# The gelu of the expert blocks computed ahead, placed one block later on ScalarE

## The chip, the cores and the metric

The kernel runs on one core of a Trainium2 chip. The metric is device microseconds of one execution, here the median of three runs. The core has five engines that run beside each other, each through its own instructions in order: TensorE (PE in the profile; its weight loads are PEld), VectorE (DVE), ScalarE (ACT), GpSimd (POOL) and SyncE (SP). An engine that waits for a semaphore holds back all that is queued behind it. ScalarE and SP also issue DMAs; those stand in the same queues as their other instructions. TensorE writes its results into PSUM, which ScalarE and VectorE read.

## What is computed

Two trunk layers over 512 latent and 256 context tokens of width 1024: a state-space mixer, then latent attention, each followed by a PEER channel mixer that picks 16 of 16384 experts for each of 8 heads. The change concerns PEER alone:

```
def peer_channel(h, w_q, keys, u_tab, v_tab):
    idx, gate = peer_route(t, w_q, keys)          # 8 heads x 16 experts for each token
    def block(args):
        hb, ib, gb = args
        act = jax.nn.gelu(jnp.einsum('td,tkd->tk', hb, u_tab[ib]), approximate=False) * gb
        return jnp.einsum('tk,tkd->td', act, v_tab[ib])
```

## The kernel before

For four token tiles of 128 tokens in the first layer and three in the second, PEER is computed densely: for each of 128 blocks of 128 experts, s = U h for all these tokens, gelu(s), times a gate matrix that is zero where a token has not picked the expert, times V. The other tiles (two and one) gather their experts' rows by indirect DMA (`gather`, lines 1233 to 1272). U, V and the activations are split into a high and a low fp32r part, so that three products stand for one: `split` (lines 302 to 305) casts the high part on ScalarE (L304) and subtracts on VectorE (L305). Line numbers L304 and L305 in the profile are therefore those of a helper, and the tile's name tells what is cast.

**Blocks ahead.** The products s = U h need neither the routing nor the gates. So 40 blocks of the first layer and 48 of the second (A0, A1) are computed ahead, while the tokens are still being routed and the gate matrices made: `ahead` (L1116 on). For each block it loads U (512 KB, on SP's queue), casts Uh (L304) and makes Ul (L305), runs 24 matmuls into one PSUM tile `s_ps` (L1110), applies the gelu on ScalarE (L1113) and stores the result `ge` to HBM (`ged`, L1123, a DMA issued by ScalarE). `pipeline(steps, LA)` with LA = 2 traces the load and split of block b+2 immediately ahead of the products of block b. In the dense stage `dense` (L1132 on) loads `ged` back (L165) in place of computing the block.

**Beside them.** `route` (L931 on) finds the top 16 on VectorE for each tile, `gate_matrix` (L1031 on) makes one-hots `e` on VectorE (L1053), casts them to `o` on ScalarE (L1058, L1064) and on VectorE (L1061), multiplies them on TensorE into `g_ps` (L1075), copies these out of PSUM on ScalarE (L1077) into `stage` and stores that to `gm` (L1079, a DMA of ScalarE's queue). The dense stage loads `gm` as `Gt`. `merge` interleaves these generators by the costs that they yield. In `peer`, `most` stops the blocks ahead three short of their number (TL = 3); the last three are traced at the beginning of `dense`.

**Order.** A planner turns the traced program into one queue for each engine. It may move an instruction ahead of earlier ones of its engine that its own timing takes to be ready later. `keep_in_program_order(x)` takes that freedom from one instruction: x then comes behind the instruction that was traced just before it on the same engine. All PSUM tiles share one pool of eight buffers (L113); U, Uh, Ul, the one-hots and other 4 KB tiles share a pool of 20.

Of the kernel before, what the change touches and what calls it, by code (L numbers as in the profile page):

```python
# [14 lines left out]
AF = mybir.ActivationFunctionType  # L15
# [70 lines left out]
def pipeline(steps, ahead):  # L86

    got = []
    for n in range(len(steps) + ahead):
        if n < len(steps):  # L90
            got.append(steps[n][0]())
        if n >= ahead:
            yield steps[n - ahead][1](got[n - ahead])
            got[n - ahead] = None
# [12 lines left out]
class Net:  # L107
# [992 lines left out]

    def dense_u(self, Us):

        PE, S = self.nc.tensor, self.nc.scalar
        TD = len(self.tiles) * 128
        Uh, Ul = Us
        sp = self.ps([128, TD], "s_ps")
        n = 0
        for k in range(KD):
            for x, y in ((Uh, 0), (Uh, 1), (Ul, 0)):
                PE.matmul(out=sp, lhsT=x[:, k, :], rhs=self.Hs[:, y, k, :], start=(n == 0), stop=(n == 3 * KD - 1))  # L1110
                n += 1
        ge = self.t2([128, TD], "ge")
        S.activation(out=ge, in_=sp, func=AF.Gelu)  # L1113
        return ge

    def ahead(self, l, n, n_tiles):  # L1116

        NT = len(self.tiles)
        self.n_ahead, self.n_done = n, 0
        self.ged = self.dram.tile([n, 128, NT * 128], F32, name=f"ged{l}")  # L1120

        def work(b, Us):
            self.nc.scalar.dma_start(out=self.ged[b], in_=self.dense_u(Us))  # L1123
            self.n_done = b + 1
            return 5.2 * NT / 4

        while len(self.qT) < n_tiles:
            yield 1.0
        yield from pipeline([(lambda b=b: self.dense_u_prep(l, b, self.nc.vector), lambda Us, b=b: work(b, Us))
                             for b in range(n)], LA)  # L1130

    def dense(self, l):  # L1132

# [453 lines left out]
```

## Time and profile before

| | us |
|---|---|
| median of 3 runs | 4093.73 |
| lowest and highest run | 4090.12, 4096.3 |
| profiled execution | 4102.76 |
| its span, first to last instruction | 4101.0 |

The rows of the profile are those of the one profiled execution. A row of the timeline gives start in us, duration in us, engine, line, operation, output tile and inputs, shapes and number of instructions merged; in brackets stands how long the engine was idle before it and what released it ("<-PE s_ps L1110": the matmul of line 1110 that writes s_ps). A row of the waits list gives the waiting engine, tile and line, whom it waited for, and then microseconds in total, number of times and the longest. A row of the windows gives the stretch and its length in us, the busy us (and instructions) of PE, PEld, DVE, ACT and POOL in this order, the TensorE clock granted as a share of full speed, and the share and GB/s of the DMA engines.

### The profile page before, as it was taken

The numbers are of one execution on the slowest core, as the hardware profiler recorded it, in microseconds if no ns is written. First come the engines' busy times: TensorE is split into PE (matmuls) and PEld (weight loads), VectorE is DVE, ScalarE is ACT, GpSimd is POOL, SyncE is SP. The second block draws the span as 40 slices with busy tenths as digits, with TensorE's granted clock in tenths as the row PEclk, the third lists the DMA queues.
The fourth block names the chain that finished last, engine by engine and source line by source line (L and its number), as shares of the span: only waits on it lengthen the run. The fifth ranks groups of instructions, "written<-read, shape, count | busy, mean of one in ns | idle before, by whom it ended". The sixth has DMA issues, their size and how long they took to land.

```text
span 4101.0 us, 53725 instructions
## 1 busy us (share of the span) xinstructions
PE 3714.2 (91%) x18955; PEld 3028.3 (74%) x18955; DVE 3140.5 (77%) x6364; ACT 1468.5 (36%) x2653; POOL 1205.7 (29%) x940
## 2 busy tenths in 40 slices
PE   6759999888679999999999989998887899999998
PEld 3437768677667878788888855568887778989997
DVE  9784387976867788989898844439977678888888
ACT  1221123366622232233332243323466333333333
POOL 5733000022413455556555300000012113333341
PEclk7879999899989999999999999999999999999999
DMA  5457244377887899999999820144377888887976
GB/s 182 137 172 250 79 132 152 100 238 249 290 311 284 294 336 354 341 358 337 341 335 346 300 98 3 44 157 137 123 239 240 310 274 316 294 339 279 343 288 217
DMA packets 398447, 986.14 MB, mean 240 GB/s; under 512 B 67040, under 2 KB 147424, under 8 KB 393568
## 3 DMA queue, kind: packets, MB, share of 16 engines
q1 hardware_dynamic: 217120, 501.34, 35.3%
q0 software_dynamic: 110592, 402.70, 27.7%
q10 hardware_dynamic: 70464, 78.65, 5.5%
q8 instruction: 149, 2.44, 0.2%
q14 instruction: 122, 1.00, 0.1%
HBM read 892.28 MB, written 90.21 MB: 240 GB/s over the span
## 4 chain that ended last, share of the span: by engine, by line
PE 54%; issue 15%; DVE 14%; POOL 7%; DMA 6%; ACT 2%; SPq 1%; POOLq 0%; ACTq 0%; DVEq 0%
PE s_ps L1110 19%; PE acc L1180 14%; POOL row L1248 6%; PE qp L919 4%; PE op L790 3%; DMA row<-in_peer_v,idx 2%; PE g_ps L1075 2%; PE zp L761 2%; DMA W<-in_peer_v 1%; DVE Ul L305 1%; PE op_mla L1480 1%; DMA ge<-ged 1%; DVE w L644 1%; PE yp L696 1%; DVE Ws L305 1%
## 5 line engine op out<-in xcount | busy, mean ns | idle before, releaser
L1180 PE MATMUL acc<-Ws,A 128*128 128x512 f32 x5208 | 1203.0, 392 | 62.7 <-ACT A L304 39.2
L1110 PE MATMUL s_ps<-Hs,Uh 128*128 128x512 f32 (+1 forms) x4096 | 1186.7, 371 | 9.2 <-ACT Uh L304 9.2
L1180 PEld LDWEIGHTS acc<-Ws,A 128*128 128x128 f32 x5208 | 982.0, 189 | 279.4 <-ACT A L304 40.0
L1248 POOL DMA_INDIRECT row<-in_peer_u,idx x384 | 512.5, 1335 | 2139.8 <-DVE row L1255 1271.8
L1110 PEld LDWEIGHTS s_ps<-Hs,Uh 128*128 128x128 f32 x4096 | 762.6, 190 | 103.8 <-ACT Uh L304 11.1
L1110 PE MATMUL s_ps<-Hs,Ul 128*128 128x512 f32 (+1 forms) x2048 | 758.3, 370 | 20.5 <-DVE Ul L305 20.5
L1248 POOL DMA_INDIRECT row<-in_peer_v,idx x384 | 483.9, 1260 | 548.2 <-DVE f L1260 477.6
L1260 DVE SCALAR_TENSOR_TENSOR f<-row,act,f 128x1024 f32<-128x1024 f32 x381 | 487.2, 1279 | 38.0 <-DMA row<-in_peer_v,idx 36.6
L1255 DVE SCALAR_TENSOR_TENSOR row<-row,m 128x1024 f32<-128x1024 f32 x384 | 461.3, 1218 | 38.8 <-DMA row<-in_peer_u,idx 38.0
L304 ACT CAST Ws<-W 128x512 fp32r<-128x512 f32 x512 | 306.2, 619 | 496.9 <-DMA W<-in_peer_v 443.3
L305 DVE TENSOR_TENSOR Ul<-U,Uh 128x1024 fp32r<-128x1024 f32 x256 | 312.0, 1220 | 175.0 <-ACT Uh L304 172.5
L1110 PEld LDWEIGHTS s_ps<-Hs,Ul 128*128 128x128 f32 x2048 | 389.5, 190 | 71.6 <-DVE Ul L305 24.8
L305 DVE TENSOR_TENSOR Ws<-W,Ws 128x512 fp32r<-128x512 f32 x512 | 345.2, 684 | 109.4 <-ACT Ws L304 108.7
L304 ACT CAST Uh<-U 128x1024 fp32r<-128x1024 f32 x256 | 267.7, 1048 | 299.8 <-DMA U<-in_peer_uT 231.7
L1075 PE MATMUL g_ps<-o,o 128*128 128x128 f32 x1792 | 241.3, 294 | 114.3 <-ACT o L1058 72.0
L1113 ACT ACTIVATE ge<-s_ps 128x512 f32<-128x512 f32 (+1 forms) x256 | 139.1, 544 | 545.8 <-PE s_ps L1110 518.2
L1075 PEld LDWEIGHTS g_ps<-o,o 128*128 128x128 f32 x1792 | 230.7, 207 | 126.1 <-ACT o L1058 124.5
L304 ACT CAST A<-ge 128x512 fp32r<-128x512 f32 (+1 forms) x256 | 144.5, 565 | 262.8 <-DVE ge L1161 257.7
L1161 DVE TENSOR_TENSOR ge<-ge,Gt 128x512 f32<-128x512 f32 (+1 forms) x256 | 155.6, 619 | 74.3 <-ACT ge L1113 48.6
L305 DVE TENSOR_TENSOR A<-ge,A 128x512 fp32r<-128x512 f32 (+1 forms) x256 | 158.3, 619 | 45.2 <-ACT A L304 44.3
L1058 ACT CAST o<-e 128x1024 f32<-128x1024 bf16 x112 | 117.3, 1048 | 88.6 <-DVE e L1053 85.5
L1077 ACT COPY stage<-g_ps 128x512 f32<-128x512 f32 x224 | 125.6, 584 | 62.3 <-PE g_ps L1075 60.8
(332 smaller groups left out, 4034.1 us busy)
## 6 DMA issues: line engine op xcount, KB each, us to landing
U<-in_peer_uT SPq DMA_DIRECT2D x256, 512.0 KB
W<-in_peer_v SPq DMA_DIRECT2D x512, 256.0 KB
gm<-stage ACTq DMA_DIRECT2D x28, 2048.0 KB
ada_wt<-in_ada_w SPq DMA_DIRECT2D x96, 512.0 KB
Gt<-gm SPq DMA_DIRECT2D x16, 2048.0 KB
Gt<-gm SPq DMA_DIRECT2D x16, 1536.0 KB
wq<-in_peer_w_q SPq DMA_DIRECT2D x40, 512.0 KB
wo<-in_s_w_o SPq DMA_DIRECT2D x48, 256.0 KB
```

Of the source, the lines that this page charges most:

```text
L304: self.nc.scalar.copy(out=hi, in_=x)
L305: lo_eng.tensor_tensor(out=lo, in0=x, in1=hi.bitcast(F32), op=ALU.subtract)
L919: PE.matmul(out=st["p"][:, h % 2, i * 128:(i + 1) * 128], lhsT=W[:, k, :], rhs=st[i][:, k, :], start=(k == 0), stop=(k == KD - 1))
L1075: PE.matmul(out=gp[:, t, :], lhsT=o[1][:, t4 * 4 + t, :], rhs=o[0][:, t4 * 4 + t, :], start=True, stop=True)
L1077: S.copy(out=stage[:, :, c:c + 4], in_=gp.rearrange("p t i -> p i t"))
L1110: PE.matmul(out=sp, lhsT=x[:, k, :], rhs=self.Hs[:, y, k, :], start=(n == 0), stop=(n == 3 * KD - 1))
L1113: S.activation(out=ge, in_=sp, func=AF.Gelu)
L1161: V.tensor_tensor(out=gv, in0=gv, in1=Gt[b // SB][:, :, :, b % SB, :], op=ALU.mult)
L1180: PE.matmul(out=acc[hf][d], lhsT=A[b][:, x, c], rhs=Ws[:, y], start=(j == 0 and n == 0), stop=(j == SB - 1 and n == 2))
L1248: GP.indirect_dma_start(out=r, out_offset=None, in_=tab, in_offset=bass.IndirectOffsetOnAxis(ap=ik[:, k:k + 1], axis=0), element_offset=l ...
L1255: x = V.scalar_tensor_tensor(out=r, in0=r, scalar=1.0, in1=m, op0=ALU.mult, op1=ALU.mult, accum_out=act[:, k:k + 1])
L1260: x = V.scalar_tensor_tensor(out=f, in0=r, scalar=act[:, k:k + 1], in1=f, op0=ALU.mult, op1=ALU.add)
```

## The change

The gelu is taken out of `dense_u` into `dense_ge`, the products into `dense_s`. In `ahead`, the gelu of a block and its store are traced behind the products of the next block, and the gelu is kept in program order. The blocks of the dense stage call both in turn as before.

```diff
     def dense_u(self, Us):
 
-        PE, S = self.nc.tensor, self.nc.scalar
+        return self.dense_ge(self.dense_s(Us))[0]
+
+    def dense_ge(self, sp):
+        ge = self.t2(list(sp.shape), "ge")
+        return ge, self.nc.scalar.activation(out=ge, in_=sp, func=AF.Gelu)
+
+    def dense_s(self, Us):
+        PE = self.nc.tensor
         TD = len(self.tiles) * 128
         Uh, Ul = Us
         sp = self.ps([128, TD], "s_ps")
...
-        ge = self.t2([128, TD], "ge")
-        S.activation(out=ge, in_=sp, func=AF.Gelu)
-        return ge
+        return sp
...
+        behind = []
+
+        def gelu(n, sp):
+            ge, x = self.dense_ge(sp)
+            self.tc.keep_in_program_order(x)
+            self.nc.scalar.dma_start(out=self.ged[n], in_=ge)
+
         def work(b, Us):
-            self.nc.scalar.dma_start(out=self.ged[b], in_=self.dense_u(Us))
+            behind.append((b, self.dense_s(Us)))
+            if len(behind) > 1:
+                gelu(*behind.pop(0))
             self.n_done = b + 1
             return 5.2 * NT / 4
...
         yield from pipeline([(lambda b=b: self.dense_u_prep(l, b, self.nc.vector), lambda Us, b=b: work(b, Us))
                              for b in range(n)], LA)
+        gelu(*behind.pop())
```

## Rows read from the trace of the kernel before

**Rows 1.** The page: span, and busy time and share of each engine.

```profile
span 4101.0 us, 53725 instructions
...
PE 3714.2 (91%) x18955; PEld 3028.3 (74%) x18955; DVE 3140.5 (77%) x6364; ACT 1468.5 (36%) x2653; POOL 1205.7 (29%) x940
```

**Rows 2.** Windows: PE, PEld, DVE, ACT and POOL, then clock and DMA.

```profile
660.00:820.00 160.00, 137.34 (x663) 110.59 (x662) 156.53 (x762) 60.10 (x85) 1.88 (x2) 0.93 0.34 104
820.00:1110.00 290.00, 229.03 (x1409) 203.35 (x1408) 215.59 (x258) 191.53 (x349) 84.25 (x56) 0.93 0.77 252
...
1400.00:2300.00 900.00, 896.11 (x3882) 728.98 (x3881) 803.67 (x1021) 273.60 (x417) 493.77 (x378) 1.00 0.94 341
2780.00:2960.00 180.00, 153.06 (x948) 145.64 (x947) 168.20 (x780) 74.46 (x116) 4.70 (x5) 0.92 0.41 133
2960.00:3180.00 220.00, 182.43 (x1215) 179.25 (x1214) 163.30 (x256) 145.25 (x259) 37.71 (x28) 0.95 0.70 231
```

**Rows 3.** Timeline, first layer: last gate store, and the first dense product.

```profile
1108.34 0.37 ACTq L1079 DMA_DIRECT2D gm<-stage  x1
...
1148.76 0.79 PE L1180 MATMUL acc<-Ws,A 128*128 128x512 f32 x1 [24.34 <-ACT A L304]
```

**Rows 4.** Waits of ScalarE, stretches 660:820, 820:1110, 2780:2960 and 2960:3180.

```profile
ACT ge L1113 <- PE s_ps L1110: 64.8, 19, 5.3
...
ACT ge L1113 <- PE s_ps L1110: 35.8, 12, 5.0
...
ACT ge L1113 <- PE s_ps L1110: 42.4, 18, 5.3
...
ACT ge L1113 <- PE s_ps L1110: 24.7, 15, 3.3
```

**Rows 5.** Waits of TensorE, stretches 660:820, 820:1110 and 2780:2960.

```profile
PE s_ps L1110 <- ACT Uh L304: 1.6, 1, 1.6
...
PE g_ps L1075 <- ACT o L1058: 43.8, 31, 6.3
...
PE s_ps L1110 <- ACT Uh L304: 7.6, 4, 2.0
```

**Rows 6.** Timeline, first layer: three pauses of TensorE behind a gelu.

```profile
941.57 0.60 ACT L1113 ACTIVATE ge<-s_ps 128x512 f32<-128x512 f32 x1 [4.99 <-PE s_ps L1110]
...
942.56 1.05 ACT L1058 CAST o<-e 128x1024 f32<-128x1024 bf16 x1 [0.40 <-DVE o L1061]
...
943.66 1.14 PE L1075 MATMUL g_ps<-o,o 128*128 128x128 f32 x5 [2.13 <-ACT o L1058]
...
972.84 2.05 PE L1075 MATMUL g_ps<-o,o 128*128 128x128 f32 x16 [0.83 <-ACT o L1058]
...
1026.50 1.27 PE L1075 MATMUL g_ps<-o,o 128*128 128x128 f32 x9 [0.77 <-ACT o L1058]
```

**Rows 7.** Timeline, second layer: a gelu, the casts behind it, and who waited.

```profile
2845.20 0.49 ACT L1113 ACTIVATE ge<-s_ps 128x384 f32<-128x384 f32 x1 [5.32 <-PE s_ps L1110]
...
2846.09 1.99 ACT L304 CAST Uh<-U 128x1024 fp32r<-128x1024 f32 x2 [0.40 <-ACT ge L1113]
2847.19 0.62 PE L1110 MATMUL s_ps<-Hs,Uh 128*128 128x384 f32 x2 [2.02 <-ACT Uh L304]
...
2858.04 1.22 DVE L305 TENSOR_TENSOR Ul<-U,Uh 128x1024 fp32r<-128x1024 f32 x1 [1.59 <-ACT Uh L304]
```

**Rows 8.** Timeline, first layer: a gelu, and the next Uh cast, which waits for U.

```profile
744.52 0.60 ACT L1113 ACTIVATE ge<-s_ps 128x512 f32<-128x512 f32 x1 [3.53 <-PE s_ps L1110]
...
748.35 1.05 ACT L304 CAST Uh<-U 128x1024 fp32r<-128x1024 f32 x1 [1.66 <-DMA U<-in_peer_uT]
```

**Rows 9.** Timeline: late Uh cast in the gate stretches, first and last pause behind one.

```profile
858.82 1.23 DVE L305 TENSOR_TENSOR Ul<-U,Uh 128x1024 fp32r<-128x1024 f32 x1 [6.89 <-ACT Uh L304]
...
863.53 0.77 PE L1075 MATMUL g_ps<-o,o 128*128 128x128 f32 x2 [5.42 <-ACT o L1058]
...
3170.09 2.28 PE L1075 MATMUL g_ps<-o,o 128*128 128x128 f32 x9 [4.41 <-ACT o L1058]
```

## What I expect, and why

> **What bounds the kernel now.** I read the page first, then the windows of the stages, then the waits of ScalarE and TensorE stretch by stretch, and last the timeline at the places the waits point to. The reader should see in the page that TensorE is busy for 91% of a span of 4101.0 us [rows 1], and in the windows that this average hides two kinds of stage. In the dense product stage (1400 to 2300 us) TensorE works 896 of 900 us at a granted clock of 1.00; nothing that ScalarE does there can shorten it. In the stages where the blocks done ahead lie, it is not full: 137 of 160 us and 229 of 290 us in the first layer, 153 of 180 and 182 of 220 in the second, at granted clocks of 0.92 to 0.95 [rows 2]. Routing and gate matrices run there, with VectorE busy 157 of 160 us while it routes and 216 of 290 us while it makes one-hots. All the work of a stage must be through before the dense products start, and TensorE is full from then on, so what a stage saves arrives at the end of the kernel.
>
> The end of each of these stages is the store of the last gate matrix: the store is issued at 1108.34 us, and the first dense product starts at 1148.76 us after TensorE stood idle for 24.34 us [rows 3]. Three ahead blocks run in between and hide under that wait. So the question is what brings the last gate store forward.
>
> **What the change does, part by part.** Today ScalarE's queue has, per block: cast of U, then the gelu, which sits until the block's 24 products are done, then the store of ged, then the next cast. The waits list puts ScalarE's idle time in front of the gelu at 64.8 us (19 times), 35.8 (12), 42.4 (18) and 24.7 (15) in the four stretches, 167.7 us together [rows 4]. Behind it in the same queue wait the Uh casts, the o casts of the gates, the copies out of PSUM and the stores of gm. The change traces the gelu of block b after the products of b+1 and pins it behind the ScalarE instruction traced just before, which is the Uh cast of b+3 (pipeline with LA = 2 runs prep(b+3) immediately before work(b+1)). It adds no instruction: as many gelus, stores and products as before, 40 blocks and 48. The order of TensorE, VectorE and SP is not named in the change; the loads on SP keep their order, and each ged store on ScalarE's queue moves one block later. The first reader of ged is the dense stage, hundreds of microseconds on for all but the last blocks, so that costs nothing; the last gelu has no later cast to wait for, and the 24.34 us of idle time behind it cover it if it slips by a microsecond [rows 3].
>
> Most of the 167.7 us is free today, because TensorE is working on the very products that ScalarE waits for. Only the part that reaches TensorE counts. I followed each TensorE pause over 0.5 us in the two stages back to what released it, and kept those whose chain goes through a gelu.
>
> First layer. One wait for a Uh cast that stood behind a gelu, 1.62 us [rows 5]. One wait for an o cast: the gelu waits 4.99 us, the o cast follows it at 942.56, and the gate products start at 943.66 after 2.13 us of pause [rows 6]. Two more of that kind, 0.83 and 0.77 us [rows 6]. Sum 1.62 + 2.13 + 0.83 + 0.77 = 5.35 us. The other pauses of the gate stretch, the greater part of 43.8 us [rows 5], have other causes: o casts behind PSUM copies, and one-hots that VectorE made late.
>
> Second layer. Four waits of TensorE for a Uh cast, 7.6 us together [rows 5]. One stands here: gelu at 2845.20 after 5.32 us of waiting, two casts behind it at 2846.09, products at 2847.19 after 2.02 us [rows 7]. With the gelu out of the way both casts could start when their U has landed, well before. Besides, VectorE waits 1.59 us for a Uh cast in front of the last steps of a routing on which the gate transposes wait [rows 7]; I count these 1.6 us once. Sum 7.6 + 1.6 = 9.2 us. These fall while VectorE routes; they count because TensorE takes blocks and gates in one order and has to be through all of them before the last gate product. Were routing alone the pace, the 7.6 would be worth nothing.
>
> Together 5.35 + 9.2 = 14.5 us. Against it stand two costs that the trace does not show, so I bound them. (a) The gelu (0.60 us, and 0.4 us until the next instruction starts behind the store's issue) must still stand somewhere; it may fall in front of an o cast that TensorE wants. At best never, 0; at worst at each of the 27 gelus that wait in the two gate stretches (12 and 15), 27 us. Today, in the first layer, it reached TensorE in 3 places; the value nearest to that is 2 us for both layers, which I take. (b) The gelu now waits behind the landing of U of b+3. ScalarE did once wait 1.66 us for a U to land [rows 8]. While it waits, TensorE has the next block to do; nearest value 0, upper end in the rival on banks below. Net gain 14.5 - 2 = 12.5 us.
>
> The profiled execution took 4102.76 us, 0.22% above the median of 4093.73. I take the 12.5 us from the execution, which gives 4090.3, and the same off the median, which gives **4081 us** (0.3% faster).
>
> **Rivals.**
>
> No change. ScalarE's wait only changes its name. The copies of g_ps out of PSUM stand in the same queue, and TensorE makes g_ps after the products in its own order; so where the gelu waited, the copy waits, and the casts behind it come as late as now. For it: at 941.57 the gelu is released and TensorE goes on at once with work that was queued; most gelu waits cost TensorE nothing. Against it: the four casts in [rows 5, 7] stand behind a gelu directly, with no copy between. The time: 4093.7 less 0 to 6, so 4086 to 4102 with what a new order of the queues may shift.
>
> Faster by more. A Uh cast that comes late makes VectorE wait, then the one-hots, then the o cast, then TensorE: VectorE waits 6.89 us at 858.82 and TensorE 5.42 us at 863.53 [rows 9]. There are eight such pauses over 4 us in the two gate stretches, 45.8 us together; the 5.42 us is the first in time and 4.41 us at 3170.09 the last [rows 9]. If half of that went too, the kernel would gain 23 us more: 4058. Against it: in front of these casts there stands a PSUM copy that waits for TensorE, and the change does not move it.
>
> Slower: PSUM banks. All PSUM tiles share one pool of eight (line 113). Today a block's bank is freed as its products end; afterwards it is held until U of b+3 has landed and been cast. In the stretch at 744.52 the gelu would come behind the cast of 748.35, so at 749.4 instead of 744.5, 4.9 us later [rows 8]: one bank more in use for most of a block's time. From the point at which a ninth bank is asked for, TensorE waits up to 4.9 us, 2.5 on average. This decides from 5 blocks on (5 times 2.5 eats the 12.5 us). If a quarter of the 37 gelus that wait in the two routing stretches (19 and 18) [rows 4] meet it, 9 times 2.5 is 23 us of loss, net 10 slower: 4104; with half of them 4126. For it: routing takes banks in pairs beside the blocks and gates. Against it: the lists of TensorE's waits in the four stretches name the o and Uh casts and VectorE's o and Ul, never a reader of a PSUM tile [rows 5], so banks are not short today. The Trainium skill, page "Perfetto Trace Analysis", section "Optimization Strategy", says that the same gap repeating on the engine that should be saturated can mean that there isn't enough SBUF or PSUM for the next tile; the pauses of this trace differ in length and in releaser, so it does not apply to the kernel before, and by that rule equal pauses in front of the products would be the mark of this rival afterwards.
>
> The change does not do what it says. The pin names one instruction, the one traced before; what is traced later may still go in front, and what stood before may stay. If the casts of b+3 were already in front of the gelus everywhere, nothing would move; the casts that follow a gelu directly [rows 7] speak against it. It would give 4094 and lies within the case of no change.
>
> **How the numbers follow.** Net gain of about 8 to 25 us, the forecast: 0.39. More than that: 0.10. Within 8.2 us of the time before (0.2%, about what a measurement of this kernel can tell from no change): 0.32. Slower by more: 0.19, by banks or by a new order of the queues that is worse by chance. Faster is then 0.39 + 0.10 = 0.49. The range goes from the upper gain, 4058, less 2, to a quarter of the blocks meeting a full pool, 4104, plus 2: 4056 to 4106. Below lie some 0.06 and above some 0.13.
>
> **What would show it.** Right: ScalarE's idle time in front of the gelu in the four stretches falls from 167.7 us to under 40; TensorE's waits for Uh casts of 1.6 and 7.6 us go; the last gate store comes about 4 us earlier in the first layer, and the same store in the second layer about 12 us earlier; the dense stage keeps its length. No change: ScalarE's idle time is found again at the copies of g_ps or at U, and the gate stores come when they did. Banks: TensorE waits for a gelu or a copy that frees a bank. My sum is wrong if the gate store moves by much more or less than the pauses I counted, which would say that a change of order, not the gelu's own wait, decides.

## The result, and the profile after

The changed kernel took 4115.48 us (median of 4 runs, 4114.32 to 4116.36), the kernel before beside it 4095.02 us (4090.12 to 4096.94): a ratio of 1.0052 [1.0034, 1.0069]. It is slower by 20 us, where 4081 us was forecast and 4106 was the upper end of the range. The profiled execution took 4116.36 us.

The page of after shows the same work in a longer span, against [rows 1] (ScalarE has two table loads less):

```profile
span 4114.6 us, 53725 instructions
...
PE 3712.9 (90%) x18955; PEld 3031.1 (74%) x18955; DVE 3136.7 (76%) x6364; ACT 1462.1 (36%) x2651; POOL 1204.2 (29%) x940
```

The waits of ScalarE and TensorE after, in the stretches of [rows 4] and [rows 5] (us in total, times, longest). First ScalarE in 660:820, 820:1110, 2780:2960 and 2960:3180, then TensorE in 820:1110 and 2780:2960:

```profile
ACT ge L1107 <- PE s_ps L1117: 7.0, 3, 3.5
...
ACT stage L1077 <- PE g_ps L1075: 52.1, 66, 4.3
...
ACT ge L1107 <- PE s_ps L1117: 5.1, 5, 2.5
...
ACT stage L1077 <- PE g_ps L1075: 56.2, 48, 5.5
...
PE g_ps L1075 <- ACT o L1058: 43.2, 31, 6.3
...
PE s_ps L1117 <- DVE Ul L305: 17.2, 7, 4.4
...
PE s_ps L1117 <- ACT Uh L304: 0.8, 1, 0.8
```

The change does what it says: ScalarE waits 12.1 us (7.0 + 5.1) for a gelu, where it was 167.7 [rows 4]. But TensorE's wait for the o casts is 43.2 against 43.8 us [rows 5], and the 7.6 us that it waited for Uh casts [rows 5] fell to 0.8 while the wait for VectorE's Ul rose to 17.2 us (11.6 before). In the same four stretches the wait for copies of g_ps rose from 60.7 to 156.3 us. The wait changed its name.

Where the time came in: I followed the starts of the stages in the two profiles. From the first product of the blocks ahead to the last gate store, the first layer took 444.3 us before and 440.9 after. The first dense stage took 1212.9 and 1220.1 us, through longer pauses; a second profile of each (below) has 1212.5 and 1215.9. Of all the profiles taken, the five whose first layer is traced as before have 1210.5 to 1218.2 for this stage, the five with the change's first layer 1212.7 to 1221.0, so whether the change lengthens it can't be told. The second layer took 377.4 and 390.8 us between the same two points, 376.2 and 390.8 in the second profiles: this is the loss, and it repeats. It lies late. Up to the first gate store after is 2 to 5 us ahead; between the fifth and the last gate store it loses 13.5 us:

Windows of TensorE from the fifth to the last gate store of the second layer (columns as in [rows 2]), before and then after:

```profile
3047.35:3177.80 130.45, 106.52 (x734) 104.80 (x733) 93.25 (x105) 89.44 (x163) 26.31 (x19) 0.96 0.77 255
```

```profile
3050.85:3194.80 143.95, 112.83 (x736) 110.49 (x735) 93.26 (x105) 89.98 (x164) 26.42 (x20) 0.92 0.70 228
```

The same 734 products (736 by the records), so 130.45 - 106.52 = 23.9 us idle before and 31.1 after, +7.2; and 6.3 us more busy, as the granted clock, a mean over the stretch, is 0.92 instead of 0.96. Windows cut more finely show where it is low. Before, it stands at the lower of TensorE's two levels (0.50 of full speed, 1.2 instead of 2.4 GHz) in 3104.70:3111.40 and 3169.60:3172.80; after, in 3098.20:3105.00, 3115.30:3122.00, 3166.50:3173.20 and 3187.00:3190.20. TensorE had just stood still each time: its pauses of over 4 us end at 3106.53 and 3170.09 before, and at 3100.87, 3116.32, 3167.31 and 3186.83 after. I call this stretch the last seven gate stores; most of the experiments are read from it.

What the added idle time is can be seen at one block. Timeline of after, from a copy of g_ps on:

```profile
3093.77 0.58 ACT L1077 COPY stage<-g_ps 128x512 f32<-128x512 f32 x1 [3.40 <-PE g_ps L1075]
3094.66 0.58 ACT L1077 COPY stage<-g_ps 128x512 f32<-128x512 f32 x1 [0.31 <-PE g_ps L1075]
3095.14 1.05 ACT L304 CAST Uh<-U 128x1024 fp32r<-128x1024 f32 x1
3096.09 0.49 ACT L1107 ACTIVATE ge<-s_ps 128x384 f32<-128x384 f32 x1
3096.22 1.22 DVE L305 TENSOR_TENSOR Ul<-U,Uh 128x1024 fp32r<-128x1024 f32 x1 [6.98 <-ACT Uh L304]
...
3098.51 1.22 DVE L1053 TENSOR_TENSOR e<-iota,iT 128x2048 bf16<-128x2048 bf16 x1
...
3099.76 1.05 ACT L1058 CAST o<-e 128x1024 f32<-128x1024 bf16 x1 [3.18 <-DVE e L1053]
...
3100.87 1.43 PE L1075 MATMUL g_ps<-o,o 128*128 128x128 f32 x5 [6.24 <-ACT o L1058]
```

The same cast (block 38) in the kernel before:

```profile
3085.61 1.05 ACT L304 CAST Uh<-U 128x1024 fp32r<-128x1024 f32 x1
...
3086.70 1.23 DVE L305 TENSOR_TENSOR Ul<-U,Uh 128x1024 fp32r<-128x1024 f32 x1 [3.25 <-ACT Uh L304]
...
3088.24 0.49 ACT L1113 ACTIVATE ge<-s_ps 128x384 f32<-128x384 f32 x1 [1.58 <-PE s_ps L1110]
...
3089.13 0.59 ACT L1077 COPY stage<-g_ps 128x512 f32<-128x512 f32 x1 [0.40 <-PE g_ps L1075]
3090.03 0.59 ACT L1077 COPY stage<-g_ps 128x512 f32<-128x512 f32 x1 [0.31 <-PE g_ps L1075]
...
3091.61 2.05 PE L1075 MATMUL g_ps<-o,o 128*128 128x128 f32 x16 [1.62 <-ACT o L1058]
```

Before, the cast stands in front of two copies of g_ps and of the gelu. After, it stands behind these two copies, which wait 3.40 us for products that TensorE makes behind a block's 24. VectorE, in order, waits 6.98 us for the cast, the one-hots behind it come late, the cast of o waits 3.18 us for them, and TensorE pauses 6.24 us. Counted through ScalarE's queue, the cast of block 38 stands behind 186 copies before and 188 after, that of block 44 behind 210 and 212; at block 44 the pause is 6.24 us again. In the whole stretch the pauses of 0.5 to 3 us shrink from 13.0 to 8.7 us, as the change meant them to, and those over 3 us grow from 10.95 (6.54 and 4.41) to 22.1 us (6.24, 5.12, 6.24, 4.48). VectorE's and TensorE's queues hold the same operations and tiles in the same order in both kernels from 2962 us on; in this stretch only ScalarE's order differs.

A second thing I had not foreseen stands just ahead of that stretch. Timeline of after:

```profile
3023.17 0.38 ACTq L1079 DMA_DIRECT2D gm<-stage  x1
...
3023.59 1.04 ACT L304 CAST Uh<-U 128x1024 fp32r<-128x1024 f32 x1 [0.45 <-ACT stage L1077]
...
3024.54 0.48 ACT L1107 ACTIVATE ge<-s_ps 128x384 f32<-128x384 f32 x1
...
3025.05 3.79 ACTq L1133 DMA_DIRECT2D ged<-ge  x1
3028.88 0.37 ACT L1043 CAST iT<-tr_ps 128x256 bf16<-128x256 f32 x1 [3.60 <-issue]
...
3029.28 1.23 DVE L1053 TENSOR_TENSOR e<-iota,iT 128x2048 bf16<-128x2048 bf16 x1 [3.40 <-ACT iT L1043]
...
3031.75 1.62 PE L1075 MATMUL g_ps<-o,o 128*128 128x128 f32 x6 [8.90 <-DVE o L1061]
```

The block's store (192 KB) is issued 1.9 us behind that of a gate matrix (2048 KB on the page) and takes ScalarE 3.79 us instead of the usual 0.33. The transposed indices wait, and TensorE pauses 8.90 us where it was 5.42 before:

```profile
3028.01 1.83 PE L1075 MATMUL g_ps<-o,o 128*128 128x128 f32 x7 [5.42 <-DVE o L1061]
```

### The profile page after: what moved, and what is told of

Its sections match the earlier page's. It is cut to its first block, busy times and chain, and to the rows that moved or that the text cites. A ratio compares the mean times of both kernels' runs of the same rounds, so it can differ in the third digit from the quotient of the medians.

```text
span 4114.6 us, 53725 instructions
## 1 busy us (share of the span) xinstructions
PE 3712.9 (90%) x18955; PEld 3031.1 (74%) x18955; DVE 3136.7 (76%) x6364; ACT 1462.1 (36%) x2651; POOL 1204.2 (29%) x940
## 3 DMA queue, kind: packets, MB, share of 16 engines
q0 software_dynamic: 110592, 402.70, 27.7%
## 4 chain that ended last, share of the span: by engine, by line
PE 56%; DVE 15%; issue 15%; POOL 6%; DMA 5%; ACT 2%; SPq 0%; ACTq 0%; POOLq 0%; DVEq 0%
PE s_ps L1117 19%; PE acc L1196 16%; POOL row L1264 6%; PE op L790 3%; PE qp L919 3%; PE g_ps L1075 2%; DMA W<-in_peer_v 2%; PE zp L761 2%; DVE Ul L305 1%; PE op_mla L1496 1%; DMA row<-in_peer_v,idx 1%; DVE w L644 1%; PE yp L696 1%; DVE rw L949 1%; DVE tk_tmp L947 1%
```

## The experiments

Ratios are to the kernel before, run beside it on the same chip. "Idle" and "length" are TensorE's in the last seven gate stores of the second layer, "casts" the copies of g_ps ahead of the casts of blocks 38 and 44 in ScalarE's queue.

| kernel | median us | ratio | idle | length | casts |
|---|---|---|---|---|---|
| before, again | 4098.11 | 0.9995 [0.9985, 1.0006] | 23.9 | 132.5 | 186, 210 |
| change, again | 4116.65 | 1.0032 [1.0019, 1.0046] | 31.1 | 143.6 | 188, 212 |
| first layer only | 4107.20 | 1.0002 [0.9993, 1.0012] | 23.9 | 137.2 | 186, 210 |
| second layer only | 4115.56 | 1.0025 [1.0014, 1.0036] | 31.1 | 143.5 | 188, 212 |
| late, not pinned | 4127.14 | 1.0057 [1.0041, 1.0074] | 33.5 | 147.2 | 187, 211 |
| own block, pinned | 4114.51 | 1.0025 [1.0009, 1.0042] | 31.1 | 143.7 | 188, 212 |
| change, store on SP | 4108.07 | 1.0016 [1.0006, 1.0027] | 31.1 | 144.3 | 188, 212 |
| before, store on SP | 4120.65 | 1.0050 [1.0036, 1.0065] | 31.5 | 144.3 | 188, 212 |
| late from block 32 | 4111.33 | 1.0037 [1.0023, 1.0052] | 31.1 | 144.0 | 188, 212 |
| own from block 32 | 4105.61 | 1.0016 [1.0006, 1.0026] | 24.5 | 137.0 | 187, 210 |
| change, casts early | 4109.69 | 1.0029 [1.0018, 1.0040] | 27.7 | 138.6 | 184, 208 |
| before, casts early | 4102.00 | 1.0010 [1.0001, 1.0020] | 21.4 | 132.1 | 184, 208 |
| casts early, store on SP | 4101.27 | 1.0006 [0.9996, 1.0015] | 23.8 | 135.3 | 184, 208 |
| first layer only, store on SP | 4092.21 | 0.9986 [0.9975, 0.9996] | 23.9 | 132.5 | 186, 210 |

**One layer at a time.** The late gelu in one layer only, by `late = int(l == 0)` or `int(l == 1)`:

```diff
-            self.tc.keep_in_program_order(x)
+            if late:
+                self.tc.keep_in_program_order(x)
...
-            if len(behind) > 1:
+            if len(behind) > late:
...
```

> The change in the first layer only (40 blocks); the second layer traces and frees its gelus as before. In the profile of the changed kernel the last gate store of the first layer came 3 us earlier and its dense products started 4.6 us earlier, but its dense stage was 7 us longer; the second layer's gate stretch was 13 us longer. Theory 'the loss is made in the gate stretch of the second layer': this kernel is at 4090 to 4098, no slower than before. Theory 'both layers lose, the first one in its dense stage': 4100 to 4105.

> The change in the second layer only (48 blocks). Theory 'the loss is made in the gate stretch of the second layer': 4108 to 4116, the whole loss, and the last gate store of the second layer is 13 us or more later after the start of its blocks. Theory 'both layers lose': 4100 to 4106.

The first layer's part alone can't be told from no change; the second layer's part alone loses 0.25%. The first of these two showed something else. Its second layer has before's queues, and its ten pauses over 0.5 us after 3020 us are before's to 0.01 us each, 29.35 us together; yet that profiled execution, the longest of its ten, took 137.2 us for the last seven gate stores:

```profile
3056.28:3193.48 137.20, 113.27 (x734) 111.44 (x733) 93.29 (x105) 89.66 (x163) 27.28 (x20) 0.90 0.74 246
```

So the granted clock alone (0.90 against 0.96) is worth 6.8 us here. I therefore read the idle time rather than the length.

**The two halves of the edit.** Late without the pin, and at its own block with the pin:

```diff
-            self.tc.keep_in_program_order(x)
```

```diff
-            if len(behind) > 1:
+            if len(behind) > 0:
...
```

> The gelu and its store are traced one block later as in the change, but the gelu is not kept in program order. Theory 'the place behind the cast of the block after next is the cause' (the gelu and its store come directly behind that cast, and the cast often comes directly behind the store of a gate matrix): without the pin the planner may put the gelu elsewhere, ScalarE's idle time in front of the gelu comes back in part, and the time is 4092 to 4102. Theory 'the later trace position alone is the cause': 4110 to 4118, as the change.

> The gelu is traced behind its own block's products as before, and kept in program order, so it comes behind the Uh cast of block b+2 in place of b+3. Theory 'the pin is the cause': this loses too, 4105 to 4115. Theory 'the later trace position is the cause': near the time before, 4090 to 4098, with ScalarE idle in front of the gelu as before (some 160 us in the four stretches).

Both lose, the free one most (its first layer takes 452 us instead of 444 besides). With the pin, the place one block later or not makes no difference to the last seven stores. So either half of the edit brings the loss without the other; what the lossy kernels share is that the two casts stand one or two copies later than before. One copy is enough: in the free one they stand behind 187 and 211, and the pauses there are 5.35 us each.

**The store on SP's queue.** The same edit in the change and in the kernel before, with both once more as they are:

```diff
-            self.nc.scalar.dma_start(out=self.ged[n], in_=ge)
+            self.nc.sync.dma_start(out=self.ged[n], in_=ge)
```

> The kernel before, unchanged, profiled once more, to tell what two profiles of one kernel differ by in the second layer's stretch from its first dense product to its last gate store (377 us in the first profile of before, 388 in the one with the first layer alone changed, 391 in the change). If that stretch varies by itself by 10 us, the loss can't be read from one pair of profiles; if it is again 377 to 380, the extra 10 to 14 us are the work of the change. Time 1.000 of before.

> The change itself, on the same chip as the three others, so that each is set against it in the same hour. Expected 1.003 to 1.007 of before, the long issues of the block stores (those over 1 us) again 9 to 13, together 25 to 35 us of ScalarE.

> The change, with one edit: the store of the gelu's block is issued on SyncE's queue instead of ScalarE's. Theory A (the loss is ScalarE held while it issues a block's store 1 to 3 us behind the 2 MB store of a gate matrix): no such hold is left on ScalarE, the pause of 8.90 us of TensorE in the second layer is back at the 5.4 of before or lower, and the time falls by 5 to 15 us against the change (0.999 to 1.003 of before). Theory B (the loss is the order of the copies, casts and products, with TensorE at the lower clock more often): the time stays at 1.004 to 1.007 of before. A third outcome, slower than the change, would be the load queue: SyncE waits for the gelu in front of the next loads.

> The kernel before with the same one edit, the store on SyncE's queue, as the control. In before's profile three of the block stores are held for over 1 us on ScalarE (3.4, 1.9 and 2.0 us, of which the first and the last stand at the ends of their stretches), so theory A expects at most 2 us of gain here (0.9995 to 1.000); theory B expects none. If SyncE's wait for the gelu costs loads, it shows here as a loss that has to be taken off the run with both.

The two repeats settle that 376 and 391 us for the second layer are not one profile's chance. With the store on SP the change gives back half of its loss in the medians (the two intervals overlap a little). Timeline of that kernel, at the place of the 8.90 us:

```profile
3015.86 1.04 ACT L304 CAST Uh<-U 128x1024 fp32r<-128x1024 f32 x1 [0.44 <-ACT stage L1077]
3016.81 0.48 ACT L1107 ACTIVATE ge<-s_ps 128x384 f32<-128x384 f32 x1
...
3017.19 0.64 ACT L1043 CAST iT<-tr_ps 128x256 bf16<-128x256 f32 x2
...
3020.53 2.69 PE L1075 MATMUL g_ps<-o,o 128*128 128x128 f32 x11 [5.41 <-DVE o L1061]
```

ScalarE is not held and the pause is before's 5.4 us; the last seven stores are unchanged, 31.1 us idle. So theory A is right for 3.5 us here; in the last seven stores it is as theory B has it. The control missed what both theories expected, and tells most: with the gelu traced where it always was, the store's queue alone puts the casts of blocks 38 and 44 behind 188 and 212 copies, and the pauses of 6.25, 5.12 and 6.25 us are there. Timeline of the control at block 38:

```profile
3086.43 0.59 ACT L1077 COPY stage<-g_ps 128x512 f32<-128x512 f32 x1 [0.31 <-PE g_ps L1075]
3086.91 1.05 ACT L304 CAST Uh<-U 128x1024 fp32r<-128x1024 f32 x1
...
3087.99 1.23 DVE L305 TENSOR_TENSOR Ul<-U,Uh 128x1024 fp32r<-128x1024 f32 x1 [6.99 <-ACT Uh L304]
...
3092.63 1.64 PE L1075 MATMUL g_ps<-o,o 128*128 128x128 f32 x6 [6.25 <-ACT o L1058]
```

The late gelu is not needed for this loss; the place of the casts comes with it. The store on SP has a price of its own besides, the one that the control's expectation names: SP now waits for a gelu in front of the next loads. ScalarE waits for U to land 18.9 us in 660:1110 of the control and 20.4 in 2780:3180, where it was 2.2 and none before; in the change it goes from 8.4 and 1.7 to 18.6 and 25.3 us. In the last seven stores neither kernel waits for U. The control's first layer is also 6 us longer (449.9), so its whole loss is not that of the two casts alone.

**Which blocks.** The late gelu only for blocks 32 to 47 of the second layer, and for all but these (`late = lambda b: l == 1 and b >= 32`, or `l == 0 or b < 32`):

```diff
-            self.tc.keep_in_program_order(x)
+            if late(n):
+                self.tc.keep_in_program_order(x)
...
-            if len(behind) > 1:
+            while behind and (behind[0][0] < b or not late(behind[0][0])):
                 gelu(*behind.pop(0))
...
```

> The late, pinned gelu only for the second layer's blocks 32 to 47, all else as before. VectorE's queue is then that of before and ScalarE's casts 38 and 44 stand behind 188 and 212 copies, as in the change. Theory C: the last seven gate stores take 143 to 145 us with 31 us of idle time, all before that is as in before, time 1.003 to 1.004 of before. A theory that needs the routing part or VectorE's changed queue expects the 130 to 133 us of before and a time of 1.000.

> The change, but with the gelu of blocks 32 to 47 of the second layer back at its own block, unpinned. VectorE's queue is that of the change; ScalarE's cast 44 is back behind 210 copies, cast 38 behind 187. Theory C: one or both of the 6.24 us pauses go, idle time of the last seven stores 24 to 27 us, their length 130 to 138 us; the store held for 3.8 to 4.5 us at 3025 us remains; time 0.999 to 1.002 of before. Theory D: idle time 23 to 25 us and 0.998 to 1.000. If the loss sat in VectorE's changed queue, idle time stays at 31 us and the time at 1.003.

Late from block 32 on, with VectorE's order that of before:

```profile
3040.73:3184.75 144.02, 112.89 (x737) 110.56 (x737) 93.28 (x105) 89.63 (x163) 26.42 (x20) 0.92 0.70 230
```

That is the whole loss of this stretch, 144.02 us and 31.1 idle, with nothing changed ahead of it and VectorE's queue as it was. The other half of the pair keeps VectorE's queue of the change. There the cast of block 44 is back behind 210 copies, its pause is gone and before's pauses follow (2.17, 1.62, 1.62, 4.40, 1.62); block 38, at 187, still costs 5.35 us. Idle time is 24.5 us as expected. The clock stayed low (0.91, 112.5 us busy), so the length is 137.0, and the store held at 3017 us is there (pause 9.05 us).

**The casts by themselves.** Blocks 38 and 44 are loaded and cast one step earlier, in the change and in the kernel before:

```diff
+        def prep(b):
+            got = pre.pop(b) if b in pre else self.dense_u_prep(l, b, self.nc.vector)
+            if l == 1 and b + 1 in (38, 44):
+                pre[b + 1] = self.dense_u_prep(l, b + 1, self.nc.vector)
+            return got
...
-        yield from pipeline([(lambda b=b: self.dense_u_prep(l, b, self.nc.vector), lambda Us, b=b: work(b, Us))
-                             for b in range(n)], LA)
+        yield from pipeline([(lambda b=b: prep(b), lambda Us, b=b: work(b, Us)) for b in range(n)], LA)
```

> The change, with one edit: of the second layer's blocks ahead, 38 and 44 are loaded and cast one step earlier, so that their Uh casts stand on ScalarE behind copy 184 and copy 208 of g_ps instead of 188 and 212 (before: 186 and 210). Theory C (in the last seven gate stores of the second layer the loss comes from these two casts, put by the planner behind two copies that wait for products, whereupon VectorE waits 7 us for each, the one-hots come late, and TensorE pauses 6.24 us twice): both pauses go, TensorE's idle time in that stretch falls from 31.1 us to 18 to 21, its length from 144 us to 126 to 133, and the time falls by 10 to 16 us against the change (0.999 to 1.001 of before). Theory D (the late gelu and its store themselves, standing in front of the casts of o): the idle time stays at 29 to 32 us and the time at 1.003 to 1.005 of before.

> The kernel before with the same edit, as the control: its casts 38 and 44 stand behind 186 and 210 copies and move to 184 and 208. In before the two long pauses of that stretch (6.54 and 4.41 us) hang on casts 40 and 46, which this edit moves little. Both theories: idle time of the last seven stores 22 to 25 us against 23.9, length 128 to 134 us, time 0.999 to 1.001 of before. If it were faster by more than that, the gain of the run with both would be the early cast's own and not the end of a loss.

The control came out as expected in length and time, with an idle time of 21.4 us a little under the 22 to 25. The change with early casts did not: idle 27.7 us instead of 18 to 21. The two pauses of 6.24 us are gone, and two others stand there. Timeline of the first:

```profile
3076.49 0.38 ACTq L1079 DMA_DIRECT2D gm<-stage  x1
3076.91 1.05 ACT L304 CAST Uh<-U 128x1024 fp32r<-128x1024 f32 x1 [0.45 <-ACT stage L1077]
3077.86 0.86 ACT L1107 ACTIVATE ge<-s_ps 128x384 f32<-128x384 f32 x2
...
3078.38 3.63 ACTq L1133 DMA_DIRECT2D ged<-ge  x2
3082.04 1.04 ACT L1058 CAST o<-e 128x1024 f32<-128x1024 bf16 x1 [3.32 <-DVE o L1061]
...
3083.14 1.22 PE L1075 MATMUL g_ps<-o,o 128*128 128x128 f32 x4 [7.30 <-ACT o L1058]
```

The early cast now stands right behind a gate matrix's store, two gelus and two stores follow, and these two hold ScalarE 3.63 us. (The bracket names VectorE for the cast of o; the time goes into the issue just ahead.) The control pauses 5.72 us at these two places, with the early cast and without a held store. So most of the 7.30 us comes from the early place itself, and 1.6 us from the held stores (1.5 at the second pause, 7.19 us). The time is near that of theory D, but the reason is not D's: what stands in front of the cast of o is the issue of the stores, not the gelus (0.86 us for two). The edit therefore does not put the casts back where they were before; it gives them a third place, with pauses of its own.

**Both at once, and the first layer without the holds.** Early casts with the stores on SP; and the late gelu in the first layer alone, with its stores on SP:

```diff
...
-            self.nc.scalar.dma_start(out=self.ged[n], in_=ge)
+            (self.nc.sync if late else self.nc.scalar).dma_start(out=self.ged[n], in_=ge)
...
```

> The change with both edits: blocks 38 and 44 loaded and cast one step earlier, and the block stores issued on SyncE's queue. If the late casts and the held stores are together the loss of the second layer: no pause over 6.5 us is left from 3020 us on, the pause at the start of the second half is 5.4 us as in before, idle time of the last seven gate stores 18 to 22 us (31.1 in the change, 27.7 with the early casts alone, 23.9 in before), their length 126 to 134 us, time 0.998 to 1.000 of before. If the late gelu itself costs something besides: idle time over 25 us and a time over 1.001.

> The late, pinned gelu in the first layer alone, with its stores on SyncE's queue; the second layer as in before, its casts 38 and 44 behind 186 and 210 copies again. The first layer's stretch from the first product to the last gate store takes 439 to 441 us (444 in before, 439.2 with this edit in both layers), the second layer's 376 to 378 us or, at the lower clock seen once with the first layer's part alone, 388. Time 0.998 to 1.000 of before by the gain of 3 to 5 us; if the gain is lost again by the end of the dense stage, 0.9995 to 1.001.

```profile
3038.41:3173.69 135.28, 111.48 (x739) 109.74 (x738) 93.00 (x104) 90.36 (x164) 25.33 (x18) 0.91 0.74 244
```

With both, idle time is 23.8 us (before: 23.9), no pause is over 5.71 us, and the second layer takes 378.1 us against 376.2 and 377.4. That is the second layer of before up to 1 or 2 us. But the fair measure is the kernel before with the same early casts: it has 21.4 us of idle time and takes 375.7 us, so 2.4 us are left that the two causes don't explain. The changed kernel with its casts behind 186 and 210 copies, as in before, was not run. I had expected 18 to 22 us of idle time, but the cast behind the gate store still makes VectorE wait 4.2 us, twice. The last kernel is the only one whose interval lies below the one before, by 7 us in the medians (0.9986 [0.9975, 0.9996]). Its first layer takes 439.7 us against 443.8 and 444.3, its second is as before (376.4); its profiled execution, 4103.3 us, is one of its three longest, with a first dense stage of 1221.1 us, so the other 3 us can't be placed.

## Why the prediction failed, point by point

**The bound.** Right for the second layer: its last gate store came 17 us later (3177.8 and 3194.8) and the kernel ended 13.6 us later in the profiles. That what a stage saves arrives at the end is not shown for the first layer: its last gate store came 3.0 us earlier (1108.34 and 1105.32), and the dense stage behind it was 7 us longer in this pair of profiles and 3 us in the second.

**The gain of 14.5 us.** Here the step that failed is "only the part that reaches TensorE counts": I took the pauses whose chain goes through a gelu as gone, without asking what is late next. The gelu's wait did go, and the pauses stayed. First layer, 5.35 us forecast: idle time fell by 1.0 us in the routing stretch and rose by 2.6 in the gate stretch (61.0 to 63.6), where the wait for VectorE's part of o rose from 17.1 to 20.4 us. From the first product to the last gate store it came 1 to 3 us shorter only because TensorE was busy for less time on as many products (360.7 and 360.0 us before, 355.7 and 357.1 after); the granted clock of the stretch reads 0.93 before and 0.93 and 0.92 after, so why stays open. Second layer, 9.2 us forecast: TensorE's waits for Uh and Ul together were 19.2 us in 2780:2960 and are 18.0. The casts came earlier, and VectorE, full with routing, was late next with Ul.

**Cost (a).** Taken at 2 us, with 0.4 us for the store's issue, and the store's later place was put at nothing. The place in the queue behind the Uh cast is in 11 cases the place right behind a gate matrix's store, where an issue takes up to 7.98 us. The block stores (L1133, before L1123) took ScalarE 58.9 us in all, against 35.2 before. The trace of before has three issues over 1 us (3.42, 1.90 and 2.02); my sum left them out. After has eleven, and one of these alone cost TensorE the 3.5 us that the run with the store on SP gave back.

**The order.** The larger failure is what has no term in my sum: "the order of TensorE, VectorE and SP is not named in the change". ScalarE's order of the casts against the copies is not named either, and it moved: even without the gelus, their stores and the table loads, 118 places of ScalarE's queue hold another operation or tile than before, and so do 310 of VectorE's and 74 of TensorE's. Two casts behind two more copies cost 11.1 us of long pauses where the short ones gave 4.3, and the lower clock 6 us more. That the place of a cast decides, and not the gelu, is shown by the kernel before with only its store moved; late from block 32 on shows that nothing ahead of these blocks and no change of VectorE's queue is needed. With both causes taken away the idle time is that of before, and 2.4 us above that of its own control. The prediction had named this sign of a wrong sum: gate stores that move otherwise than the pauses counted, because a change of order decides.

**The rivals.** "No change" told the mechanism right (the wait is found again at the copies of g_ps) and the time wrong, since the pauses moved with it. "Faster by more" named the very chain that lost: cast late, VectorE waits, one-hots late, TensorE pauses. I read it only as something to be gained, and held against it that the change does not move the copy in front of these casts; the order of the two did move. The 6.89 us at 858.82 [rows 9] was also the price of one more such cast, but "a new order of the queues that is worse by chance" only shared 0.19 with the banks and had no price. "PSUM banks" did not come: no list of TensorE's waits names a gelu or a copy that frees a bank. "Does not do what it says" is refuted by the 12.1 us.

**Left open.** Why the planner puts the two casts there was not tried; three different edits gave the same place. Nor is it settled why the granted clock of the same pauses is 0.96, 0.94 or 0.90 in different executions; some 6 us of the second layer's loss stand on it. All seven profiles with the casts behind 188 and 212 copies have 0.91 or 0.92 there. Whether the change lengthens the first dense stage, by 3 to 7 us in the two pairs of profiles, is open as well.

## What to carry to other kernels

When a planner orders the queues, price a moved instruction not by the wait that it had, but by one slip of its neighbours: find the longest chain in the trace of before (a late cast, two engines behind it, a pause of 5 to 6 us) and ask how many more of it the new order could make. An in-order engine's wait for another engine is worth nothing until you have seen that the next thing in its queue could run. Before you place a DMA on a compute engine's queue, look at how long each of its issues holds that engine, and what was issued just ahead; before you move it to the queue of the loads, look at which loads would wait behind it.

## What the runs showed of the hardware

How long ScalarE took to issue a block's store hung on whether a 2 MB store of the same queue was just ahead. In after, all 11 stores issued 1.3 to 3.4 us behind one took 0.79 to 7.98 us; the 14 issued 3.4 to 12 us behind one took 0.33 to 1.82, and the 44 more than 12 us behind one 0.33 to 0.34. Before, one of 67 was within 3.4 us (1.90 us). The longest in after, 1.4 us behind the last gate store of the first layer:

```profile
1105.32 0.37 ACTq L1079 DMA_DIRECT2D gm<-stage  x1
...
1106.76 7.98 ACTq L1133 DMA_DIRECT2D ged<-ge  x1
```

The large store itself is issued in 0.37 us; the next one pays. In the change with its block stores on SP's queue, 11 of them were also issued 1.3 to 3 us behind a 2 MB store, which ScalarE still issues, and none took long. All 88 there (shortest, median and longest in ns):

```profile
L1133 SPq DMA_DIRECT2D ged<-ge x88: 319/320/612, 670.9 to 3202.1; - x88
```

The Trainium skill, page "DMA: Bandwidth & Descriptors", section "Issuing engines are not separate DMA queues", says that issuing from several engines saves only the sequencer's time to start the DMA, usually small beside the DMA itself. In these runs it was mostly small (0.33 us) and at times not (up to 7.98 us); no view of these runs gives how long these DMAs themselves took. The change with its stores on SP was 8.6 us faster in the median than with them on ScalarE, and the kernel before 22.5 us slower (both with what else that edit moved in the queues).
